# A copy by DMA ahead of the MLP's transposes, and transposes as rounded fp32

## The chip, the cores and the metric

The kernel runs on one core of one Trainium2 chip. The metric is the device time of one execution in microseconds (us), lower is better; the figure of a kernel is the median of its runs. A profiled execution leaves a trace: for each engine, each instruction with its start, its duration and what ended the idle time before it. The engines are named PE (TensorE matmul), PEld (TensorE's weight loads, which run beside PE), DVE (VectorE), ACT (ScalarE), POOL (GpSimd) and SP (SyncE); SPq, ACTq and POOLq are DMA issues by those engines.

## The reference

A decoder trunk of two layers in fp32, 256 tokens by 2048 features: layer 0 mixes tokens by latent attention, layer 1 by a state-space scan, and each is followed by a dense MLP with squared ReLU. Only the MLP matters here:

```python
def squared_relu_mlp(h, w_in, w_out):
    u = jax.nn.relu(h @ w_in)
    return (u * u) @ w_out

...
        h = rms_norm(x, mlp_norm_g[i])
        x = x + squared_relu_mlp(h, mlp_w_in[i], mlp_w_out[i])
```

`w_in` is 2048 x 8192 and `w_out` 8192 x 2048, in each layer.

## The kernel before

**Numbers.** Every operand of a matmul is split into two parts of the type fp32r (fp32 rounded for TensorE): `hi`, the rounded value, and `lo`, the rounded rest. A product is then three matmuls: hi with hi, hi with lo, lo with hi. Weights come in units of 128 x 1024 words (512 KB): SP loads a unit (L87), ACT writes its hi part `wh` (L102), DVE its lo part `wl` (L103), and PE uses both. `Flow` keeps this pipeline: at each unit it first issues loads up to six units ahead and then splits up to three units ahead.

**The MLP.** Hidden features are worked off in eight pairs of 512-column blocks, p = 0 to 7, each with two blocks j and two token tiles t of 128 tokens. Pair 0 is computed plainly. Pairs 1 to 7 use seven products in place of eight (`seven`, L170): sums of the weights' quarters are made on DVE (L183), and seven products M1, N7, N5, N6, N4, M2, N3, of four units d = 0 to 3 each, are added up into four tiles of hidden values in PSUM banks. For N7 the sum is `b22 = b12 + b22` of two units that were just loaded by SP; for N5 `b12 = b11 + b12`; for N6 `b11 = b11 + b22`, after which POOL adds another quarter by DMA (L199).

**A hidden tile.** When a tile [128 tokens x 512] is complete, DVE combines it (L598, L599), ACT applies ReLU with the norm's scale (L602) and squares it in place (L546, in `hidden`). PE then transposes it: four transposes of 128 x 128 into one PSUM bank `sm` (L310, in `transposed`), written here as one group. ACT writes the hi part of the bank's content (L299) and DVE the lo part (L300) into the tiles `k`, which the products with `w_out` (`yp<-wh,k`) read. Here the tile that is transposed is fp32, and so is the identity.

**Order.** PE's order is written out by the program: `plan()` gives a list of unit steps, in which the seven products of pair p + 1 (`st` banks) and the products with `w_out` of pair p (`yp` banks) are interleaved, and `mlp_body` walks through it. A group of transposes isn't issued when its tile is squared but becomes due later: `turn` sets the due time `us` (the table `TR`) after the present step, at least `TR_GAP` after the group before; `move` advances a counter by 1.36 or 2.72 a step, and issues what is due. The order of the other engines' instructions is decided by a scheduler when the program is built, from the order of issue and the dependences; within an engine instructions run strictly in that order.

Of the kernel before, what the change touches and what calls it, by code (L numbers as in the profile page):

```python
# [20 lines left out]
F32 = mybir.dt.float32  # L21
F32R = mybir.dt.float32r
# [6 lines left out]
P = 128  # L29
# [185 lines left out]
class Trunk:  # L215
# [90 lines left out]

    def transposed(self, src, h, lo, wide=True):
        b = self.bank(wide)
        for j in range(4):
            self.nc.tensor.transpose(b[:, j * P:(j + 1) * P], src[:, j * P:(j + 1) * P], self.ident)  # L310
        self.split_out(h, lo, b.rearrange("p (k n) -> p k n", k=4))


# [225 lines left out]
    def mlp_body(self, mp, layer, gain):  # L539
        nc = self.nc  # L540
        xa, rs = self.xT, self.rs
        us = {}

        def hidden(r, pp, j, t):

            nc.scalar.activation(r, r, AF.Square)  # L546
            if (pp, j) not in us:
                us[pp, j] = (self.ktile(self.k4), self.ktile(self.k4))
            h, lo = us[pp, j]
            return lambda wide: self.transposes(r, h, lo, t, wide)  # L550

        def relu(src, t):
# [12 lines left out]
        out, bank, v, count = {}, {}, {}, {}  # L565
        due = []
        at = [0.0, 0.0]
# [10 lines left out]
        def turn(r, p, j, t, us):  # L578

            fn = hidden(r, p, j, t)  # L580
            at[1] = max(at[0] + us, at[1] + TR_GAP)
            due.append((at[1], lambda: fn(False)))

        def pair_of_banks(pool):
# [20 lines left out]
        def after(name, p):  # L605
            if name == "M1":
                v["m1"] = self.scratch()
                nc.scalar.activation(v["m1"], bank["M1"], AF.Copy)
            elif name in ("N5", "N6"):
                v[name] = p  # L610
                if v.get("N5") != p or v.get("N6") != p:
                    return
                w, c, e = (self.scratch() for _ in range(3))
                sub(w, bank["N6"], v["m1"])
                plus(c, bank["N5"], w)
                plus(w, bank["N7"], w)
                plus(e, bank["N7"], c)
                v["w"], v["c"] = w, c
                turn(relu_in_place(e, 1), p, 1, 1, TR[0])
            elif name == "N4":  # L620
                sub(v["w"], bank["N4"], v["w"])
                turn(relu_in_place(v["w"], 1), p, 0, 1, TR[1])
            elif name == "M2":
                plus(v["m1"], bank["M2"], v["m1"])
                turn(relu_in_place(v["m1"], 0), p, 0, 0, TR[2])
            elif name == "N3":
                plus(v["c"], bank["N3"], v["c"])
                turn(relu_in_place(v["c"], 0), p, 1, 0, TR[3])
# [5 lines left out]
        for tok in tokens:  # L634
            key = (tok[0], layer) + tok[1:]
            if tok[0] == "s":
                _, p, name, d = tok
# [12 lines left out]
            elif tok[0] == "c":  # L650
                _, p, j, o = tok
# [11 lines left out]
            else:  # L663
                _, p, nb, o = tok
# [701 lines left out]
LATE5 = ()  # L1366
TR = (10, 8, 7, 7, 5)
TR_GAP = 4
PAUSE = 2.7


def merged(p, blocks):
# [21 lines left out]
    while main or late or second or units:  # L1394
        op = next((q for q in (late, main, second) if q and ready(*q[0])), None)
        filler = t >= rest and len(units) > (4 if p == 7 and op else 0)
        if filler and (op is None or work > t * ve / pe - 2):
# [3 lines left out]
            if not units or units[0][0] != b:  # L1401
                rest, work = t + (PAUSE if b[0] == "o" else 10), work + 1.37
        else:
# [160 lines left out]
```

## Time and profile before

| | |
|---|---|
| median of 3 runs | 2296.01 us (2294.32 to 2296.62) |
| profiled execution, time | 2298.62 us |
| profiled execution, span of the core | 2296.8 us |
| mean granted TensorE clock | 0.999 |
| PE busy | 2285.9 us |
| DVE busy | 1908.8 us |
| ACT busy | 1393.0 us |
| moved by DMA | 538.07 MB |

The span runs from the first to the last instruction of the core; 1.8 us of the execution's time lie around it. A row of a group reads: line of the code, engine, operation, output tile and input tiles, shape, count, busy time in us and the mean duration of one in ns, then the engine's idle time just before them and what ended most of it. A row of a timeline reads: start and duration in us, engine, line, operation, tiles, shape, count of instructions put together, and in brackets the idle time before it and who ended it. Durations of matmuls are modelled ends, since matmuls are pipelined: their pace is read from the distance of the starts. Line numbers are those of the kernel before; in the changed kernel L310 is L312, L546 is L550, L599 is L607, and L419 is L421.

### The profile page before, as it was taken

Reading aid. Unit: us, or ns where it says so; the run is one execution under the profiler, and the core shown is the slowest. Engines: PE = TensorE matmul, PEld = TensorE weight load, DVE = VectorE, ACT = ScalarE, POOL = GpSimd, SP = SyncE. Lnnn points to the kernel's source line nnn. Section 1 sums busy time; section 2 is a strip of 40 time slices with the busy share of each in tenths; the row PEclk is TensorE's granted clock in tenths of the full one; section 3 lists DMA queues with packets and bytes.
Section 4 is the critical chain, followed back from the end, with each engine's and each line's share of the span. In section 5 each row is a group of like instructions: output and inputs, shape, how many; then the busy total and the mean of one; then the engine's idle time right before and its main releaser. Section 6 shows DMA issues by size and latency. Waiting matters only on the chain.

```text
span 2296.8 us, 30456 instructions
## 1 busy us (share of the span) xinstructions
PE 2285.9 (100%) x10929; PEld 1899.3 (83%) x10929; DVE 1908.8 (83%) x2318; ACT 1393.0 (61%) x1947; POOL 213.1 (9%) x229
## 2 busy tenths in 40 slices
PE   9999999999999999999999999999999999999999
PEld 7898888888888888888887888888888888888887
DVE  7786697999899898687888688676989989989895
ACT  7775475566566666564665555545666666666663
POOL 1430000000000000000122212110000000000000
PEclk9999999999999999999999999999999999999999
DMA  8445687887887878667877777666687788888775
GB/s 316 149 126 158 198 232 240 264 241 252 265 242 245 263 213 277 202 207 243 283 262 245 250 260 261 227 196 203 210 256 232 249 263 246 243 271 239 246 232 163
DMA packets 161912, 538.07 MB, mean 234 GB/s; under 512 B 17680, under 2 KB 26832, under 8 KB 160736
## 3 DMA queue, kind: packets, MB, share of 16 engines
q1 hardware_dynamic: 151264, 502.44, 66.0%
q0 software_dynamic: 8096, 29.41, 7.9%
q10 hardware_dynamic: 2400, 4.27, 0.5%
q8 instruction: 86, 1.41, 0.3%
q14 instruction: 66, 0.54, 0.1%
HBM read 529.65 MB, written 6.41 MB: 233 GB/s over the span
## 4 chain that ended last, share of the span: by engine, by line
PE 96%; DVE 2%; DMA 1%; issue 0%; ACT 0%; SPq 0%; POOL 0%; DVEq 0%; ACTq 0%
PE acc L325 13%; PE acc L326 13%; PE acc L329 13%; PE yp L595 9%; PE yp L596 9%; PE yp L594 9%; PE st L595 7%; PE st L596 7%; PE st L594 7%; PE sm L310 2%; DMA wraw<-mi 1%; DVE wl L103 1%; PE y L1280 1%; PE acc L594 1%; PE acc L596 1%; PE acc L595 1%
## 5 line engine op out<-in xcount | busy, mean ns | idle before, releaser
L102 ACT ACTIVATE wh<-wraw 128x1024 fp32r<-128x1024 f32 (+1 forms) x818 | 857.6, 1053 | 601.5 <-PE acc L326 285.1
L103 DVE TENSOR_TENSOR wl<-wraw,wh 128x1024 fp32r<-128x1024 f32 (+1 forms) x818 | 985.7, 1220 | 231.4 <-ACT wh L102 222.2
L595 PE MATMUL yp<-wl,k 128*128 128x512 f32 x896 | 349.1, 390 | 1.8 <-DVE wl L103 1.8
L594 PE MATMUL yp<-wh,k 128*128 128x512 f32 x896 | 349.9, 391 | 0.0
L596 PE MATMUL yp<-wh,k 128*128 128x512 f32 x896 | 348.8, 389 | 0.0
L325 PE MATMUL acc<-wh,xt 128*128 128x512 f32 x704 | 279.9, 398 | 0.8 <-ACT wh L102 0.8
L326 PE MATMUL acc<-wh,xt 128*128 128x512 f32 x704 | 274.8, 390 | 0.0
L102 ACT ACTIVATE wh<-wrx 128x1024 fp32r<-128x1024 f32 x168 | 178.0, 1059 | 135.7 <-PE yp L596 105.6
L103 DVE TENSOR_TENSOR wl<-wrx,wh 128x1024 fp32r<-128x1024 f32 x168 | 203.9, 1219 | 37.7 <-ACT wh L102 37.6
L595 PEld LDWEIGHTS yp<-wl,k 128*128 128x128 f32 x896 | 168.2, 188 | 37.7 <-DVE wl L103 3.3
L596 PEld LDWEIGHTS yp<-wh,k 128*128 128x128 f32 x896 | 168.2, 188 | 34.9
L594 PEld LDWEIGHTS yp<-wh,k 128*128 128x128 f32 x896 | 168.3, 188 | 34.8
L325 PE MATMUL acc<-wh,k 128*128 128x512 f32 x496 | 196.5, 396 | 0.0
L326 PE MATMUL acc<-wh,k 128*128 128x512 f32 x496 | 193.2, 390 | 0.0
L329 PE MATMUL acc<-wl,xt 128*128 128x512 f32 x704 | 188.3, 389 | 0.0
L594 PE MATMUL st<-wh,xt 128*128 128x512 f32 x448 | 176.8, 395 | 0.0
L595 PE MATMUL st<-wl,xt 128*128 128x512 f32 x448 | 174.8, 390 | 0.0
L596 PE MATMUL st<-wh,xt 128*128 128x512 f32 x448 | 174.7, 390 | 0.0
L325 PEld LDWEIGHTS acc<-wh,xt 128*128 128x128 f32 x704 | 132.7, 188 | 30.6 <-ACT wh L102 2.6
L326 PEld LDWEIGHTS acc<-wh,xt 128*128 128x128 f32 x704 | 132.6, 188 | 27.7 <-issue 1.2
L199 POOL DMA_DIRECT2D wrx<-mi x56 | 49.2, 878 | 1142.0 <-DVE wl L103 1035.1
L329 PEld LDWEIGHTS acc<-wl,xt 128*128 128x128 f32 x704 | 132.2, 188 | 27.7
(307 smaller groups left out, 3450.0 us busy)
## 6 DMA issues: line engine op xcount, KB each, us to landing
wraw<-mi SPq DMA_DIRECT2D x256, 512.0 KB, 5.2
wraw<-mo SPq DMA_DIRECT2D x256, 512.0 KB, 5.3
wraw<-si SPq DMA_DIRECT2D x160, 512.0 KB, 4.9
wraw<-so SPq DMA_DIRECT2D x64, 512.0 KB, 4.8
wrx<-mi SPq DMA_DIRECT2D x56, 512.0 KB, 5.2
wrx<-mi POOLq DMA_DIRECT2D x56, 512.0 KB, 8.2
wraw<-wo SPq DMA_DIRECT2D x32, 512.0 KB, 4.0
taps<-xD SPq DMA_DIRECT2D x16, 768.0 KB, 8.2
```

Source lines behind the costliest of these rows:

```text
L102: self.last = nc.scalar.activation(h[:, v], raw[:, v], AF.Copy)
L103: self.last_lo = nc.vector.tensor_tensor(lo[:, v], raw[:, v], h[:, v].bitcast(F32), ALU.subtract)
L199: nc.gpsimd.dma_start(st["b11"].tile, quarter(d, 1, 0), accum_op=ALU.add)
L310: self.nc.tensor.transpose(b[:, j * P:(j + 1) * P], src[:, j * P:(j + 1) * P], self.ident)
L325: nc.tensor.matmul(accs[t][:, :n], ah, wh[:, q, :], start=first and kt + q == 0, stop=False)
L326: nc.tensor.matmul(accs[t][:, :n], al, wh[:, q, :], start=False, stop=False)
L329: nc.tensor.matmul(accs[t][:, :n], lhs(kt + q, t)[0], wl[:, q, :], start=False, stop=en and q == nk - 1)
L594: nc.tensor.matmul(b, ah, wh, start=first and q == 0, stop=False)
L595: nc.tensor.matmul(b, ah, wl, start=False, stop=False)
L596: nc.tensor.matmul(b, al, wh, start=False, stop=last and q == 1)
L1280: nc.tensor.matmul(y[t][c, o], part(t)[:, c], xg[g][t][:, o], start=True, stop=True)
```

## The change

In pairs 1 to 6 of both layers, after a hidden tile is squared, ACT issues a DMA that copies it, word for word, into a tile `tr` of the type fp32r (four buffers). The transposes then read that tile, their identity is an fp32r copy (made once a layer by POOL), and their output bank is seen as fp32r. Groups of these pairs become due 5 later (`COPY`). Pairs 0 and 7 and all other transposes stay as they were. The DMA copies words: it doesn't round, so the values that are split into hi and lo afterwards are those of the squared tile.

```diff
     def transposed(self, src, h, lo, wide=True):
         b = self.bank(wide)
+        words = src.dtype == F32R
+        out, one = (b.bitcast(F32R), self.ident_r) if words else (b, self.ident)
         for j in range(4):
-            self.nc.tensor.transpose(b[:, j * P:(j + 1) * P], src[:, j * P:(j + 1) * P], self.ident)
+            self.nc.tensor.transpose(out[:, j * P:(j + 1) * P], src[:, j * P:(j + 1) * P], one)
         self.split_out(h, lo, b.rearrange("p (k n) -> p k n", k=4))
...
         us = {}
+        self.ident_r = mp.tile([P, P], F32R, name="identr")
+        nc.gpsimd.tensor_copy(self.ident_r, self.ident)
 
         def hidden(r, pp, j, t):
...
             h, lo = us[pp, j]
+            if pp in WORDS:
+                q = mp.tile([P, 512], F32R, tag="tr", name=self.name("tr"), bufs=4)
+                nc.scalar.dma_start(q.bitcast(F32), r)
+                r = q
             return lambda wide: self.transposes(r, h, lo, t, wide)
...
             fn = hidden(r, p, j, t)
-            at[1] = max(at[0] + us, at[1] + TR_GAP)
+            at[1] = max(at[0] + us + (COPY if p in WORDS else 0), at[1] + TR_GAP)
             due.append((at[1], lambda: fn(False)))
...
 TR = (10, 8, 7, 7, 5)
 TR_GAP = 4
+WORDS = range(1, 7)
+COPY = 5
 PAUSE = 2.7
```

## The prediction

> **What bounds the kernel now.** I read the busy shares and the chain of the page first, then a table by stretches for one steady pair of the MLP, then the timelines of single engines inside that pair.
>
> ```profile
> span 2296.8 us, 30456 instructions
> ...
> PE 2285.9 (100%) x10929; PEld 1899.3 (83%) x10929; DVE 1908.8 (83%) x2318; ACT 1393.0 (61%) x1947; POOL 213.1 (9%) x229
> ...
> PE 96%; DVE 2%; DMA 1%; issue 0%; ACT 0%; SPq 0%; POOL 0%; DVEq 0%; ACTq 0%
> ...
> 460.00:544.00 84.00, 84.00 (x380) 69.60 (x379) 77.19 (x76) 53.48 (x58) 3.51 (x4) 1.00 0.83 252
> ```
>
> TensorE sets the end: 96% of the chain. In the last row (a stretch, then busy time of PE, PEld, DVE, ACT and POOL, the granted clock, DMA share, GB/s) PE is never idle in a steady pair, at clock 1.00. But VectorE works 77.19 of the 84 us, so it leads PE by little, and what reorders DVE can stop PE. The change touches both: it shortens PE's transposes, and it reorders DVE.
>
> What one group of four transposes costs PE is read from the PE timeline (start, duration, line, tiles):
>
> ```profile
> 461.12 0.39 PE L596 MATMUL yp<-wh,k 128*128 128x512 f32 x1
> 461.35 0.60 PE L310 MATMUL sm<-cst,s 128*128 128x128 f32 x4
> 461.71 0.48 PE L594 MATMUL st<-wh,xt 128*128 128x512 f32 x1
> 462.02 0.39 PE L595 MATMUL st<-wl,xt 128*128 128x512 f32 x1
> ...
> 463.86 0.39 PE L594 MATMUL st<-wh,xt 128*128 128x512 f32 x1
> ...
> 465.90 0.39 PE L594 MATMUL yp<-wh,k 128*128 128x512 f32 x1
> ```
>
> From 463.86 to 465.90 are nine matmuls, 0.227 us each. From 461.12 to 463.86 are ten matmul steps (2.27 us) and one group: 2.74 - 2.27 = 0.47 us a group. The change turns 48 groups (four in each of pairs 1 to 6, two layers) into fp32r: 22.6 us of PE time are at stake, and only a part can be saved.
>
> **The change part by part.** *The transposes as fp32r.* No row has an fp32r matmul of 128 columns, so I bound it by fp32r matmuls of fewer columns than 512 and by the fp32 transposes (durations min/median/max):
>
> ```profile
> L310 PE MATMUL sm<-cst,s x396: 270/272/273, 49.0 to 2249.5; 128*128 128x128 f32 x198
> L344 PE MATMUL sm<-xt,wh x32: 277/283/283, 28.8 to 976.2; 128*128 128x256 f32 x32
> L325 PE MATMUL acc<-wh,cq x56: 333/334/422, 55.8 to 152.1; 128*128 128x384 f32 x56
> ...
> 72.11 0.19 PEld L325 LDWEIGHTS acc<-wh,cq 128*128 128x128 f32 x1
> 72.22 0.19 PEld L326 LDWEIGHTS acc<-wh,cq 128*128 128x128 f32 x1
> ```
>
> 128 columns fewer take 334 - 283 = 51 ns off; 128 columns of fp32r would be 283 - 51 = 232 ns against 272 now. If pitch follows duration, a transpose gains 40 ns, a group 0.16 us, 48 groups 7.7 us: the upper end. The other end is no gain: the weight loads of 128 columns in the last two rows, where the matmuls are short, come 0.11 us apart, and four loads at 0.11 are 0.44 us, about the whole group of today; if a transpose's load takes as long in fp32r, loads set the pitch and nothing is won. I take 0.135 us a group, or 6.5 us: nearer to the upper end, because the transposes' loads have shorter records now than matmuls' loads (138/140 against 188 ns, rows below), but less than all of it, because the next matmul's load no longer fits under a short transpose.
>
> ```profile
> L310 PEld LDWEIGHTS sm<-cst,s x396: 138/140/146, 48.8 to 2249.4; 128*128 128x128 f32 x198
> L325 PEld LDWEIGHTS acc<-wh,xt x704: 186/188/333, 5.5 to 1546.5; 128*128 128x128 f32 x176
> ```
>
> The Trainium skill ("TensorE: Matmul & The Clock Gate", LDWEIGHTS) has a rule that speaks against this part: a load takes its columns divided by 1.2 in ns, 107 ns for 128 columns, whatever the type. By that rule the sum would hold no PE gain; the 0.11 us spacing of the two loads agrees with it, the 140 ns records of the transposes do not decide it.
>
> *The copies.* 48 ACT-queue DMAs of 256 KB. Nearest rows for the issue and for the landing:
>
> ```profile
> L1193 ACTq DMA_DIRECT2D xD<-xtm x8: 366/368/393, 1028.1 to 1461.3; - x8
> ...
> xD<-xtm ACTq DMA_DIRECT2D x8, 512.0 KB, 6.6
> gb<-g SPq DMA_DIRECT2D x12, 256.0 KB, 2.6
> ...
> gb<-sng SPq DMA_DIRECT2D x8, 256.0 KB, 4.9
> ```
>
> Issuing costs ACT 0.37 us, four a pair 1.5 us, against 84.00 - 53.48 = 30.5 us that ACT is idle there; behind an issue stand the next weight splits (L102), which start 0.37 us later and are mostly early. Were that cover gone, it would be 48 x 0.37 = 17.8 us. The landing lies between 2.6 us and 6.6 us; I take 4.9, a transfer of this size among others. Four copies add 1 MB a pair to 252 GB/s x 84 us = 21 MB, 5%, at a DMA share of 0.83. The copies must land before the group that reads them:
>
> ```profile
> 480.88 0.62 ACT L546 ACTIVATE s<-s 128x512 f32<-128x512 f32 x1
> ...
> 483.17 0.60 PE L310 MATMUL sm<-cst,s 128*128 128x128 f32 x4
> ```
>
> This is the tightest of a pair's four: 1.67 us from the square's end to the group. COPY = 5 moves the groups; in the program order of the changed kernel the four of a steady pair stand 30, 24, 18 and 18 matmuls later, 6.8, 5.4, 4.1 and 4.1 us. So this copy has 1.67 + 4.1 = 5.8 us for 0.37 + 4.9 = 5.3 us: on time by half a microsecond, cost nothing; the other three have 0.6 us or more beyond that. The hidden tiles are first read some 50 matmuls behind the moved groups, so nothing waits there. The copies pass through no queue of the weight loads (those go by SP). The rounded identity is one small copy on POOL a layer, which is idle for 91%. These cost nothing.
>
> *DVE's order.* This is what the diff does not show. The groups' splits (L300) move with the groups, and around them the scheduler now puts the sum b12 + b22 of unit N7 (L183), which waits for a weight load, ahead of one or two weight splits (L103) that stood before it. Comparing the orders, this happens to 20 of 56 sums, ten a layer: the first of pairs 2 to 7 passes one split, the third of pairs 3 to 6 passes two. In a steady pair:
>
> ```
> before: L599, L103 wl180, L103 wl181, L183 wraw184, L300, L103 wl182
> after:  L607, L300, L103 wl180, L183 wraw184, L103 wl181, L103 wl182
> ```
>
> A sum that waits now holds back finished work that PE wants. That such sums do wait is in the view of waits:
>
> ```profile
> DVE wraw L183 <- DMA wraw<-mi: 21.1, 22, 3.0
> ...
> wraw<-mi SPq DMA_DIRECT2D x256, 512.0 KB, 5.2
> ```
>
> Place A, the first sum of a steady pair:
>
> ```profile
> 467.09 2.06 SPq L87 DMA_DIRECT2D wraw<-mi  x2
> ...
> 471.21 0.68 DVE L599 TENSOR_TENSOR s<-st,s 128x512 f32<-128x512 f32 x1
> 471.81 2.35 DVE L103 TENSOR_TENSOR wl<-wraw,wh 128x1024 fp32r<-128x1024 f32 x2
> 474.08 1.23 DVE L183 TENSOR_TENSOR wraw<-wraw,wraw 128x1024 f32<-128x1024 f32 x1
> ...
> 476.12 0.39 PE L595 MATMUL yp<-wl,k 128*128 128x512 f32 x1
> ```
>
> The second load goes out at 467.09 + 2.06 - 0.33 = 468.82 and lands 5.2 us later, at 474.0. After the change: L300 (0.6 like L599, which has the same size) until 472.4, wl180 until 473.55, the sum at 474.0 until 475.15 (1.14 from one to the next, (474.08 - 471.81)/2), wl181 ready at 476.37. PE wants it at 476.12 less 0.47, since the pair's second group has moved from before to behind it: 475.65. PE waits 0.7 us. With a load that lands by 473.55 it is 0.25 us. Half the loads are earlier than the median, so I take 0.5; ten such places (pairs 3 to 7, two layers): 5.0 us.
>
> Place B, the third sum:
>
> ```profile
> 493.90 0.33 SPq L87 DMA_DIRECT2D wraw<-mi  x1
> ...
> 494.99 3.48 DVE L103 TENSOR_TENSOR wl<-wraw,wh 128x1024 fp32r<-128x1024 f32 x3
> 498.39 1.22 DVE L183 TENSOR_TENSOR wrx<-wrx,wraw 128x1024 f32<-128x1024 f32 x1
> 499.53 1.22 DVE L183 TENSOR_TENSOR wraw<-wraw,wraw 128x1024 f32<-128x1024 f32 x1
> ...
> 501.55 0.39 PE L595 MATMUL st<-wl,sN 128*128 128x512 f32 x1
> ```
>
> The load lands at 493.9 + 5.2 = 499.1. After: the sum from 499.1, the wrx sum, then wl193: 499.1 + 1.14 + 1.14 + 1.22 = 502.6, wanted at 501.55: 1.05 us. With a load a microsecond earlier nothing. I take 0.5; eight places: 4.0 us.
>
> Pair 2, where PE already waits for the first sum:
>
> ```profile
> 387.29 1.23 DVE L103 TENSOR_TENSOR wl<-wraw,wh 128x1024 fp32r<-128x1024 f32 x1
> 390.55 1.23 DVE L183 TENSOR_TENSOR wraw<-wraw,wraw 128x1024 f32<-128x1024 f32 x1 [2.04 <-DMA wraw<-mi]
> ...
> 390.60 0.39 PE L595 MATMUL st<-wl,xt 128*128 128x512 f32 x1
> ...
> 392.96 0.50 PE L595 MATMUL yp<-wl,k 128*128 128x512 f32 x1 [0.82 <-DVE wl L103]
> ```
>
> The split of 387.29 now stands behind the sum of 390.55: ready at 390.55 + 1.14 + 1.23 = 392.9, wanted at 390.60 less 0.47: a wait of 2.75 us. It swallows the present one (six matmuls behind 390.60, at 0.23 each, is 391.99; it starts at 392.96: 0.97 us), so about 1.75 us more a layer, 3.5 us.
>
> Sum: -6.5 + 5.0 + 4.0 + 3.5 = +6.0 us. On the profiled execution that is a span of 2302.8 us and a time of 2304.6 (it took 2298.62 with 1.8 around its span); that execution lies 2.6 above the median, so I forecast 2296.0 + 6.0 = **2302 us**.
>
> **The rivals.** (1) *Faster: DVE takes up the waits.* It has 84.00 - 77.19 = 6.8 us of idle time a pair; if loads land a microsecond early at A and B and the scheduler's order costs nothing, the PE gain stays: 2296.0 - 6.5 = 2289.5, or 2293 with pair 2's. For it: place A's floor is 0.25 us, B's nothing. Against: 22 sums wait already, up to 3.0 us. It decides if the loads land under 4.7 us. (2) *The rounded type quickens nothing*, the loads set 0.11 us a transpose: 2296.0 + 12.5 = 2308.5. For it the two loads at 72.11; against it the transposes' shorter load records. This would be the change not doing what it looks like. The Trainium skill's LDWEIGHTS rule ("TensorE: Matmul & The Clock Gate") would give this rival. (3) *The copies land late.* At the 6.6 us of the xD row, the tightest needs 0.37 + 6.6 = 7.0 of its 5.8 us: 1.2 us of PE wait, in 12 pairs 14 us: 2316. It decides from a landing of 5.4 us on. For it: the transfers share a load stream with 0.83 of DMA time; against it: xD is twice the size. In the Trainium skill ("DMA: Bandwidth & Descriptors", Issuing engines are not separate DMA queues) transfers of all engines interleave on the same 16 DMA engines; the trace has no copy inside the MLP to test it. (4) *Gain and waits cancel*: half the waits, 2296.0 - 6.5 + 6.2 = 2295.7, no change.
>
> **How the numbers follow.** My forecast (2298 to 2305) 0.40; (1) 0.20; (2) 0.15; (3) 0.10; (4) 0.15. What this measurement can tell from no change is 0.2%, 4.6 us: faster is below 2291.4, slower above 2300.6. Faster: rival 1, 0.20. Within: rival 4 and a little of the forecast's lower end, 0.20. Slower: the rest, 0.60. The range goes from 2290 (rival 1 almost whole) to 2312 (rival 2 with 0.7 us at A and B alike: 7.0 + 5.6 + 3.5 = 16.1); outside lie the best of rival 1 and most of rival 3, 0.2 together.
>
> **What would show it.** The transposes' record near 232 ns and a group at 0.33 us of PE time prove the gain, 0.47 refutes it. In the waits, PE's idle time on wl from L103, 0.82 us in the row of 392.96 and its like in the other layer, must grow to some 12 us, and DVE's L183 on loads from 21 us; the stops must stand just behind first and third sums, the largest at pair 2. The copies should show 2.6 to 6.6 us to landing, and the groups no wait for DMA. If PE waits at the groups instead, rival 3 holds; if PE's idle time does not grow, I am wrong about the order on DVE, and the time falls by the PE gain.

## The result, and the profile after

The changed kernel takes 2328.27 us (median; 2326.86 to 2328.91) against 2296.19 us: ratio 1.0138 (1.0125 to 1.015), 32 us slower. The forecast was 2302 us with a range from 2290 to 2312. The direction was right, the loss is five times the 6 us of the sum.

The page of the changed kernel: span, busy times, the chain of work that ended last, and one group of matmuls with the idle time before it.

```profile
span 2326.1 us, 30526 instructions
...
PE 2294.6 (99%) x10929; PEld 1897.9 (82%) x10929; DVE 1907.2 (82%) x2318; ACT 1391.4 (60%) x1947; POOL 216.7 (9%) x231
...
PE 85%; DMA 6%; DVE 5%; issue 2%; ACT 1%; POOL 0%; SPq 0%; DVEq 0%; ACTq 0%
...
L603 PE MATMUL yp<-wl,k 128*128 128x512 f32 x896 | 352.4, 393 | 12.5 <-DVE wl L103 12.5
```

PE's share of the chain has fallen from 96% to 85%; DMA and DVE have taken its place. What PE waits for is the view of waits (who waited, for whom: us in all, times, longest):

```profile
DVE wraw L183 <- DMA wraw<-mi: 55.9, 35, 3.1
...
PE yp L603 <- DVE wl L103: 12.5, 13, 1.9
PE st L603 <- DVE wl L103: 11.4, 9, 2.6
```

In the kernel before, the same view has for PE:

```profile
PE yp L595 <- DVE wl L103: 1.8, 3, 0.8
```

DVE's wait of L183 for loads has grown from 21.1 to 55.9 us, PE's for the lo parts of weights from 1.8 to 23.9. One steady pair in the PE timeline shows where (the number in brackets is idle time):

```profile
479.78 0.50 PE L603 MATMUL yp<-wl,k 128*128 128x512 f32 x1 [1.39 <-DVE wl L103]
...
506.93 0.50 PE L603 MATMUL st<-wl,sN 128*128 128x512 f32 x1 [1.13 <-DVE wl L103]
...
525.18 0.50 PE L603 MATMUL yp<-wl,k 128*128 128x512 f32 x1 [0.28 <-DVE wl L103]
```

The first is place A of the prediction, the second place B; the third, behind the fourth sum, was not foreseen. That sum's place among the splits has not changed; the chain ahead of its stop starts with a load of 6.54 us. The chain of waits at A (start, length, what) names the mechanism in four lines:

```profile
470.99 6.25 DMA wraw<-mi
...
477.37 0.06 DVE wraw L183
...
478.51 1.23 DVE wl L103
479.78 0.50 PE yp L603
```

The load takes 6.25 us. The sum starts at its end; behind the sum comes the lo part of a weight that was already there, and behind that PE. The DVE timeline at the same place:

```profile
474.57 1.22 DVE L103 TENSOR_TENSOR wl<-wraw,wh 128x1024 fp32r<-128x1024 f32 x1
477.37 1.22 DVE L183 TENSOR_TENSOR wraw<-wraw,wraw 128x1024 f32<-128x1024 f32 x1 [1.57 <-DMA wraw<-mi]
478.51 2.35 DVE L103 TENSOR_TENSOR wl<-wraw,wh 128x1024 fp32r<-128x1024 f32 x2
```

A part of the loss is not idle time. After four of the longer stops, matmuls run at about half pace for some 3 us. From the PE timeline at pair 2, and the same stretch in the table by windows (stretch, busy of PE, PEld, DVE, ACT, POOL, granted clock, DMA share, GB/s):

```profile
392.31 0.50 PE L603 MATMUL st<-wl,xt 128*128 128x512 f32 x1 [2.37 <-DVE wl L103]
...
394.03 0.63 PE L602 MATMUL yp<-wh,k 128*128 128x512 f32 x1
394.45 0.63 PE L603 MATMUL yp<-wl,k 128*128 128x512 f32 x1
394.88 0.63 PE L604 MATMUL yp<-wh,k 128*128 128x512 f32 x1
```
```profile
393.60:396.00 2.40, 2.40 (x7) 1.92 (x6) 2.40 (x3) 1.06 (x1) 0.00 (x0) 0.50 0.82 259
397.00:400.00 3.00, 3.00 (x17) 2.48 (x16) 2.22 (x3) 1.65 (x4) 0.00 (x0) 1.00 0.54 213
```

The pitch is 0.43 us at a granted clock of 0.50, 0.227 at 1.00. There are four such stretches, each of six to nine matmuls, some eight on average: about 4 x 8 x 0.2 = 6.4 us.

The parts add up to about the whole loss. The 22 stops have 23.9 us of idle time. Each costs 0.27 more than its bracket shows (a matmul's record lasts 0.39, its pace is 0.227; the next matmul starts 0.34 behind instead of 0.227): 5.9 us. The slow matmuls are 6.4. Off go 2.9 for shorter transposes (below) and some 2.6 for the three stops that were there before. That makes 30.7 us, where the span grew by 29.3.

The transposes and copies, in the groups by form and the DMA issues:

```profile
L312 PEld LDWEIGHTS sm<-identr,tr x192: 137/139/182, 372.2 to 2194.9; 128*128 128x128 f32 x192
L312 PE MATMUL sm<-identr,tr x192: 220/239/252, 372.4 to 2195.0; 128*128 128x128 f32 x192
...
DMA to landing us min/median/max: 2.3/5.5/7.1
```

The record of one transpose fell from 272 to 239 ns, near the 232 that was extrapolated, but the time of a group fell by little. A group of the changed kernel in the timeline of PE:

```profile
470.56 0.39 PE L604 MATMUL yp<-wh,k 128*128 128x512 f32 x1
470.79 0.46 PE L312 MATMUL sm<-identr,tr 128*128 128x128 f32 x4
471.08 0.46 PE L602 MATMUL st<-wh,xt 128*128 128x512 f32 x1
...
474.83 0.39 PE L603 MATMUL st<-wl,xt 128*128 128x512 f32 x1
```

From 470.56 to 474.83 are 17 matmul steps (3.85 us) and a group: 0.42 us, and the median of all is 0.41, against 0.47 before. That is 0.06 us a group, 2.9 us in all. The loads of the same group, before and after, show where it comes from:

```profile
461.13 0.58 PEld L310 LDWEIGHTS sm<-cst,s 128*128 128x128 f32 x4
461.68 0.19 PEld L594 LDWEIGHTS st<-wh,xt 128*128 128x128 f32 x1
```
```profile
470.57 0.54 PEld L312 LDWEIGHTS sm<-identr,tr 128*128 128x128 f32 x4
471.05 0.19 PEld L602 LDWEIGHTS st<-wh,xt 128*128 128x128 f32 x1
```

From the group's first load to the next matmul's load were 0.55 us and are 0.48. Of the four distances in between, the first (0.23 us) stays; each of the other three falls from 0.108 to 0.085 us (medians of all such groups).

### The profile page after: what moved, and what is told of

The parts are those of the page before. It is cut to its first block, busy times and chain, and to the rows that moved or that the text cites. A ratio compares the mean times of both kernels' runs of the same rounds, so it can differ in the third digit from the quotient of the medians.

```text
span 2326.1 us, 30526 instructions
## 1 busy us (share of the span) xinstructions
PE 2294.6 (99%) x10929; PEld 1897.9 (82%) x10929; DVE 1907.2 (82%) x2318; ACT 1391.4 (60%) x1947; POOL 216.7 (9%) x231
## 4 chain that ended last, share of the span: by engine, by line
PE 85%; DMA 6%; DVE 5%; issue 2%; ACT 1%; POOL 0%; SPq 0%; DVEq 0%; ACTq 0%
PE acc L327 13%; PE acc L328 13%; PE acc L331 12%; PE yp L603 8%; PE yp L604 8%; PE yp L602 8%; DMA wraw<-mi 6%; PE st L603 5%; PE st L604 5%; PE st L602 5%; DVE wl L103 4%; PE sm L312 1%; PE y L1288 1%; ACT wh L102 1%; PE acc L604 1%
```

## The experiments

Three theories stood against each other. *Order*: the sums that wait for loads stand ahead of weight splits on DVE that could already run. *Traffic*: the copies slow the loads. *Place*: groups that come later make something else wait. All ratios are to the kernel before, run on the same chip. In the code, `...` stands for lines left out.

**delay.** Kernel before with `COPY = 5` in `turn`, no copies, no new type.

```diff
-            at[1] = max(at[0] + us, at[1] + TR_GAP)
+            at[1] = max(at[0] + us + (COPY if p in WORDS else 0), at[1] + TR_GAP)
...
```

> Kernel before with the groups of pairs 1 to 6 due 5 later and nothing else: no copies, fp32 transposes. On DVE the first sums of pairs 2 to 7 come out one split later than before, not earlier. Theory 'order' (the loss is made by sums that wait for loads and stand ahead of finished weight splits): no loss, 2294 to 2299 us. Theory 'place' (the later groups themselves make PE or DVE wait): 2305 us or more. Theory 'traffic' (the copies' DMA traffic delays the weight loads): 2294 to 2299 us, as there are no copies.

Measured: 2295.16 us, ratio 0.9993 (0.9984 to 1.0002). The later place of the groups costs nothing that shows. In this kernel twelve first sums come out one split later than before, so order and place change together; *heldb* below has ten of these twelve held without the late groups, and the same ratio.

**unread.** Kernel before with the copies, which nobody reads.

```diff
+            if pp in WORDS:
+                q = mp.tile([P, 512], F32R, tag="tr", name=self.name("tr"), bufs=4)
+                nc.scalar.dma_start(q.bitcast(F32), r)
             return lambda wide: self.transposes(r, h, lo, t, wide)
...
```

> Kernel before with the 48 copies added on ACT's queue, which nobody reads; transposes as before. All the copies' traffic and issue time, DVE's sums where they were. Theory 'traffic': the loads that the sums wait for land a microsecond later, 2310 us or more. Theory 'order': within 2294 to 2300 us.

Measured: 2298.79 us, ratio 1.0012 (1.0003 to 1.0021). The copies alone, traffic and issue, cost 2.9 us, not 30; no N7 sum's place among the splits on DVE has changed in this kernel.

**early.** Kernel before, in which ten first sums (place A, pairs 3 to 7) stand one weight split earlier on DVE. `sum()` is the addition `b12 + b22` of a unit of N7; three units ahead it is issued first and the splits are held behind it.

```diff
-            self.split[self.done] = self.units[self.done].make()
+            for n in range(self.done, min(self.done + 4, len(self.units))):
+                k = self.units[n].key
+                if k[0] == "s" and k[3:] == ("N7", 0) and k[2] > 2 and n == self.done + 3:
+                    self.early[n] = self.units[n].sum()
+            held = [e for n, e in self.early.items() if n > self.done]
+            with self.tc.issue_after(held[0].ins) if held else nullcontext():
+                self.split[self.done] = self.units[self.done].make()
...
```

> Kernel before, only the first N7 sum of pairs 3 to 7 is put one weight split earlier on DVE (ten sums, the place A of the prediction), nothing else. Theory 'order': the stops of 0.75 to 1.4 us that the changed kernel shows there come back, some 1.1 us each, less what loads land earlier without the copies: 2302 to 2309 us. Theory 'traffic' or 'place': 2294 to 2298 us.

Measured: 2302.07 us, ratio 1.0027 (1.0016 to 1.0038): 6.2 us, with no copy, no new type and no moved group. In the profiled execution five of the ten places have a stop, the longest (2.66 us between starts) behind a load of 7.20 us. The chain at a place A of this kernel shows the same sequence as the changed kernel's, with a load of 5.57 us in place of 6.25:

```profile
468.07 5.57 DMA wraw<-mi
...
473.77 0.06 DVE wraw L189
...
474.91 1.23 DVE wl L103
476.14 0.04 issue
476.18 0.50 PE yp L605
```

**order.** The changed kernel, with each of these sums held behind the weight split behind which it stood before. Some, the third sums among them, came out a split or two later still.

```diff
+        self.los[self.done] = self.last_lo.ins
...
             if name == "N7":
-                add("b22", "b12", "b22")
+                back = BACK.get(p, (3, 5, 4, 5))[d]
+                with flow.tc.issue_after(flow.los[flow.done - back]) if p > 1 else nullcontext():
+                    add("b22", "b12", "b22")
...
+BACK = {2: (4, 4, 4, 5), 7: (3, 4, 6, 5)}
```

> Changed kernel, copies and fp32r transposes kept, but each N7 sum of pairs 2 to 7 is held behind the weight split behind which it stood before (some come out one split later still). Theory 'order': the loss is gone, and the shorter transposes show: 2290 to 2299 us. Theory 'traffic' or 'place': 2315 us or more.

Measured: 2293.26 us, ratio 0.9991 (0.9982 to 1.0). The whole loss is gone, with copies, traffic, late groups and fp32r all in place. Its chain, and the wait of its sums for loads:

```profile
PE 97%; DVE 2%; DMA 1%; issue 0%; SPq 0%; ACT 0%; DVEq 0%
...
DVE wraw L184 <- DMA wraw<-mi: 18.5, 20, 2.3
```

No row of PE waiting for wl is left.

**hold0 and hold2.** As *order*, but the hold applies to one place alone: `if p > 1 and d == 0` and `if p > 1 and d == 2`.

> Changed kernel, only the first N7 sum of pairs 2 to 7 held behind its weight splits; the third sums of pairs 3 to 6 stay two splits early (place B). If the loss is the stops that stand in the changed kernel's trace at B (1.3, 1.4, 1.3 and 2.0 us in layer 0, and some 0.4 us just after), it is 2293.3 (the run in which all sums are held) plus 12 to 18: 2304 to 2312 us. If B was only a consequence of the delays at A, it is under 2300 us.

> Changed kernel, only the third N7 sum of pairs 3 to 6 held; the first sums of pairs 2 to 7 stay early (place A and pair 2). By the stops of layer 0 (2.5 us at pair 2, 0.9 to 1.6 us at A, and the slow matmuls behind the longest stop): 2293.3 plus 14 to 20, 2307 to 2314 us. If A and pair 2 mattered only together with B: under 2300 us.

Measured: hold0 2303.58 us, ratio 1.0028 (1.0018 to 1.0038); hold2 2319.82 us, ratio 1.0096 (1.008 to 1.0111). The kernel before took 2297.22 us on that chip, so ratios are what to compare: against *order* (0.9991), the early third sums, which *hold0* leaves, cost 0.37%, 8.5 us, and the early first sums, which *hold2* leaves, 1.05%, 24.1 us. The sum, 32.6 us, is nearly the whole distance of the changed kernel from *order* (1.0138 - 0.9991 = 1.47%, 33.8 us). hold0 came out just under the 2304 to 2312 us that were expected and hold2 above its range: first sums, pair 2 among them, are the larger part. The stops behind fourth sums are in the smaller part: *hold0* still has two of them.

**earlyun.** *early* and *unread* together.

> Kernel before with ten first sums one split early and the copies, which nobody reads. Alone the early sums cost 6.2 us and the copies 2.9 us. If the copies' traffic lengthens the waits of the early sums (loads landing at 6.3 in place of 5.1 us), stops grow to some 1.1 us each: 2307 to 2314 us. If not, the two costs add up: 2303 to 2306.5 us.

Measured: 2314.22 us, ratio 1.0072 (1.006 to 1.0085). That is 16.5 us, just above the range for lengthened waits, where the two alone make 0.27% + 0.12%, 9.0 us. The copies cost little while sums stand well, and 0.45% (10.3 us) beside early sums. The waits of PE in *early* and in *earlyun*, and the loads' landing (issues, KB, median us):

```profile
PE yp L605 <- DVE wl L103: 5.2, 7, 2.3
...
wraw<-mi SPq DMA_DIRECT2D x256, 512.0 KB, 5.1
```
```profile
PE yp L608 <- DVE wl L103: 12.3, 12, 1.5
...
wraw<-mi SPq DMA_DIRECT2D x256, 512.0 KB, 5.6
```

Half a microsecond on the loads' median makes five more stops out of places that were just in time, and the mean stop goes from 0.74 to 1.03 us. The loads that the ten first sums wait for change more than the median of all: read in the traces, from issue to landing, as the load that landed last ahead of each sum, their medians are 5.2 us in the kernel before, 5.0 in *early*, 6.2 in *unread*, and 5.9 in *earlyun* and in the changed kernel. *unread* has the late loads and no early sums, and loses little. (The profiled execution of *earlyun* is its fastest, 2309.92 us.)

**words32o, and order_b and words32o_b.** The twin of *order* with fp32 transposes: copies, places and holds stay, only the type differs. (The scheduler answers even that: the third sum of pair 7 stands one split later in each layer.)

```diff
-                q = mp.tile([P, 512], F32R, tag="tr", name=self.name("tr"), bufs=4)
-                nc.scalar.dma_start(q.bitcast(F32), r)
+                q = mp.tile([P, 512], F32, tag="tr", name=self.name("tr"), bufs=4)
+                nc.scalar.dma_start(q, r)
...
```

> The kernel with all sums held, but the copies go to an fp32 tile and the transposes stay fp32: copies, places and DVE order as there, only the type of the transposes differs. If a group of fp32r transposes saves the 0.057 us that the changed kernel's timeline shows: 2293.3 + 2.7 = 2296 us (2294.5 to 2297.5). If it saves the 0.135 us of the prediction: 2299.8 us. If nothing: 2293.3 us.

> The changed kernel with all sums held once more, beside its twin with fp32 transposes on the same chip. If a group of fp32r transposes saves 0.06 us and nothing takes it back, it is 2.9 us (0.13%) faster than the twin; if something takes it back, the two agree within 1 us. Ratio to the kernel before again 0.998 to 1.000.

> The twin with copies and fp32 transposes, all sums held, on the same chip as the one with fp32r. Theory 'the type gains': 2.9 us slower than that one. Theory 'nothing is gained': equal within 1 us.

Measured: words32o 2294.9 us, ratio 0.9992 (0.9983 to 1.0001), with no fp32r kernel measured beside it. Then both side by side: order_b 2293.62 us, 0.9983 (0.9974 to 0.9992), words32o_b 2295.19 us, 0.9989 (0.9981 to 0.9998). The type is ahead by 1.6 us in the last pair and, by ratios, by 0.2 us between the first; the intervals overlap. The times neither show nor refuse the 2.9 us of the timeline. The traces of this pair do show them in PE's time: a group takes 0.47 us in words32o_b and 0.41 in order_b (medians). The prediction's 6.5 us, 0.28%, is more than the two intervals of the last pair leave room for.

**heldb.** Kernel before with ten first sums (pairs 2 to 6) held one split longer, and nothing else.

```diff
+                back = BACK.get(p, (2, 5, 4, 5))[d]
+                with flow.tc.issue_after(flow.los[flow.done - back]) if p > 1 else nullcontext():
+                    add("b22", "b12", "b22")
...
+BACK = {2: (3, 4, 4, 5), 7: (3, 4, 6, 5)}
```

> Kernel before with nothing changed but ten first sums (pairs 2 to 6) held one weight split longer on DVE: no copies, no later groups, fp32 transposes. If the 0.1% that the held kernels are under the kernel before comes from the wait at pair 2 that goes away (0.97 us in layer 0 and its like in layer 1), it is 1 to 3 us under before here too. If it comes from the transposes, it equals before.

Measured: 2294.79 us where before takes 2297.39, ratio 0.9993 (0.9984 to 1.0002). PE's wait for wl falls from 1.8 to 0.2 us:

```profile
PE yp L599 <- DVE wl L103: 0.2, 1, 0.2
```

The size fits the wait at pair 2, but the interval holds 1: not settled. With nearly the order of *delay* and none of its late groups the ratio is the same, 0.9993, so late groups add nothing that shows.

**all8.** *order* with `WORDS = range(8)`: 64 groups.

> All sums held, copies and fp32r transposes in all pairs 0 to 7 (64 groups in place of 48). By 0.06 us a group one more microsecond is gained: 2292 to 2293 us on a chip where before takes 2296. Where the groups of pair 0 or 7, which come at once behind one another, wait for their copies, it is slower than with pairs 1 to 6, by some 5 us a pair and layer.

Measured: 2296.93 us, ratio 0.9998 (0.9989 to 1.0007): no gain. Its waits have new rows that *order* lacks, at the transposes' splits:

```profile
PE acc L331 <- DVE k L303: 1.8, 2, 0.9
...
PE acc L330 <- ACT k L302: 0.9, 2, 0.5
```

These are four waits, 2.7 us, in the products with `w_out` just behind the last pair's groups, where the later groups come too late. *order* remains the fastest kernel tried, 0.1 to 0.2% under the kernel before in both of its measurements.

## Why the prediction was wrong

**What held.** PE sets the end before; the change reorders DVE; the loss comes at the first sums, the third sums and pair 2. *early* and *order* show this, one by making it and one by removing it. Place, ACT's issues and POOL's copy cost nothing that shows (*order* keeps all three; in *unread* the copies and their issues together cost 2.9 us). PE never waited for a copy, so rival 3 is out, although the copies' landing (5.5 us median) came up to the 5.4 from which it was to decide: neither the changed kernel nor *order* has a row of PE waiting for DMA.

**What failed: places A and B.** The step was "With a load that lands by 473.55 it is 0.25 us. Half the loads are earlier than the median, so I take 0.5". It took the loads as those of the kernel before, median 5.2, and looked for the better half. Alone, that was a fair size: *early* has 6.2 us at ten places, 0.6 each, though in its profiled execution one long load makes much of it. But in the same kernel the copies lengthen just these loads, to a median of 5.9 us. With 5.9 in place of 5.2 the prediction's own working gives 0.7 + 0.7 = 1.4 us at A; the ten stops there, by the distances of starts, lose 13.3 us, and *earlyun* against *unread* gives 13.8 (1.0072 - 1.0012 = 0.60%), where the sum had 5.0. Single rows are 1.39 us of idle time at 479.78 for A and 1.13 at 506.93 for B. So the mechanism was right and its size was not: the copies' traffic was priced at nothing in one step and the sums' waits at the old loads in the next. Each was nearly right, and the two together were not. Rival 3 had the traffic on the copies' own landing, and not on the loads.

At B the sum had 4.0 us, and seven stops lose 7.6. The 1.05 us a place that the working gave with the median load is near the measured mean, 0.94 over eight places; what failed is the halving to 0.5. In layer 0 B's loads took 6.0 to 6.6 us, in layer 1 4.8 to 5.5, and the stops are long in layer 0 alone (1.5 to 2.2 us between starts, against 0.6 to 1.0). In *unread* B's loads took 4.2 to 4.7 us, so the copies alone don't explain B's late loads; their cause stays open.

**What was missing.** The slow matmuls behind four of the stops, 6.4 us, were in no term. Nor was the third stop of a pair (0.28 us of idle time in the row of 525.18); there are three such stops, 1.3 us in all.

**Pair 2** was sized right: 3.5 us more in both layers were forecast, and it is 3.6. The start at 392.31 stands 2.76 us behind the matmul before it, a wait of 2.53 where 2.75 was forecast; in layer 1 it is 3.00. A slow stretch of some 1.6 us came on top each time.

**The transposes** gained 0.06 us a group, not 0.135: 2.9 us in place of 6.5. The record went to 239 ns as extrapolated; the step that failed is "If pitch follows duration". The record is 33 ns shorter, but only three of a group's distances between loads are shorter, by 0.023 us each. The weight loads' records did not change (139 ns against 140). The Trainium skill's rule of a load time by columns, which names no type, gives 107 ns for 128 columns ("TensorE: Matmul & The Clock Gate", LDWEIGHTS); it fits the 0.108 us from load to load in fp32, but not the 0.085 us in fp32r, where the measurement decides. Rival 2, that nothing at all is won, does not hold in PE's time, since the group is 0.06 us shorter in the timeline.

**What moved the sums** is not the move of the groups alone. The prediction said that the scheduler puts the sums ahead around the splits that move with the groups. In *delay* the groups move just so, and the first sums come out later; in *unread* the copies are there, and no sum moves. Among these kernels only the whole change puts them ahead; which parts of it are needed stays open.

**The rivals that ended lower** (1 and 4) had DVE's idle time or early loads take up the waits. Neither happened: at A the lo part behind the sum starts at 478.51 and PE, already waiting, uses it at 479.78, so idle time that DVE has later cannot make the wait good; and the loads came later, not earlier.

## What to carry to other kernels

Where an engine runs in order, a change of types or times that seems to touch another engine can reorder it; compare the orders of the built programs, and look for operations that wait for loads and now stand ahead of work that could already run. When a step both puts work behind a load and adds traffic, price the wait with the load as the new traffic makes it, at the very place, and not with the median of before. If such a change is worth having for its own sake, hold the waiting operation behind the work that it passed: here one such hold a sum brought back 1.5%, 34 us.

## What the runs showed of the hardware

After a stop, PE can lose half its clock for a while: granted 0.50 for six to nine matmuls at 0.43 us, starting at once or up to 1.4 us behind the stop. It followed stops of 2.76 us at 392.31, 2.19 at 767.31, 3.00 at 1751.91 and 2.26 at 1839.67 (distance of starts in the changed kernel's timeline), but not those of 1.78 at 479.78, of 2.16 at 2011.93 and of 2.22 at 2183.13, so that the length alone doesn't decide it; what does, no run here shows.

A copy of 256 KB within on-chip memory took as long to land (5.5 us, 2.3 to 7.1) as the weights' load of 512 KB beside it (5.6 us).

Transposes in fp32r between fp32r matmuls load their weights every 0.085 us, those in fp32 every 0.108 us, though a load's record lasts the same (139 and 140 ns).
